# Summing the norms' squares on VectorE before one sum over the partitions, in a three-layer kernel on one core

## The chip, the cores and the metric

The kernel runs on one core of one Trainium2 chip. The metric is the device time of one execution in microseconds (us). TensorE multiplies matrices, VectorE (DVE in the profile) and ScalarE (ACT) work elementwise, GpSimd (POOL) and SyncE (SP) issue transfers here.

## The reference, cut to what matters

Three transformer layers work on one sequence of 256 tokens with 1024 features: stick-breaking attention, sparse attention over a latent with 16 heads, and window attention beside a gated linear recurrence. Each layer is followed by a feed-forward part with a causal convolution of three taps. Ahead of each half of a layer stands a norm over the features:

```python
y = xf * lax.rsqrt(jnp.mean(xf * xf, axis=-1, keepdims=True) + RMS_EPS)
h = rms_norm(x, norm_mix[i]) * (1.0 + sc1) + sh1
```

The sparse attention norms each of its 16 heads' queries over 128 features as well, and the window attention norms its output over 512 features. So the squares of x have to be summed over the features for every token, and the features lie on the partitions.

## The kernel before, in words

All activations are kept transposed: a tile holds 128 features on the partitions and T = 256 tokens along the free axis, and `x` is eight such tiles (`KT`). Weights stream in by DMA into `raw`; each piece is split into a high part `wh` on ScalarE (`high`) and a low part `wl` on VectorE (`low`), and each product is made of three in the float32r type (`three`): high by high, low by high, high by low. The activations are split likewise into `xh` and `xl`, `oh` and `ol`, `gh` and `gl`. A scheduler orders the instructions of each engine when the program is built; each engine then works through its own list in order.

`residual` stands at the end of each half of a layer. Its inner function `done` is called for the eight tiles in the order `ORD` (0, 2, 4, 6, 1, 3, 5, 7): VectorE adds the product to `x` (line 694), ScalarE makes `xh` (line 689) and the square `sq` (line 634), VectorE makes `xl` (line 690). After four tiles `gather` multiplies the four squares by `first_one`, a 128x32 tile whose first column is one, so that each product uses 32 columns of the array and leaves its sum over the partitions in one row of the bank `po`. After all eight, `regather` copies the bank to `part` on ScalarE (line 663) and multiplies it by `ones`, which yields one sum for each token. `rsqrt` takes these (line 647) through a logarithm, an exponential and one Newton step, and `spread` multiplies the result by the identity so that it stands on all partitions.

`opening` begins the next half of a layer meanwhile: its first three units take the split of x times its gain, without the norm's factor, and their results are scaled by the factor once it is there. `GS` says from which of these products on the sums and the spread must stand ahead of them in TensorE's list (lines 787 to 793).

The five norms handled in this way follow two kinds of half layers. Three follow an attention, so that `down_last` closes an output projection (the profile's stretches from 152, 499 and 842 us); two follow a feed-forward part (from 348 and 692 us). The very last norm (`last`, `finish`) already adds its squares on VectorE and isn't touched but for its buffers. In the sparse attention `heads` and `head_sums` do the same gathering for four groups of four heads, in the mixed layer `window` does it once.

Of the kernel before, what the change touches and what calls it, by code (L numbers as in the profile page):

```python
# [10 lines left out]
F32 = mybir.dt.float32  # L11
F32R = mybir.dt.float32r
U8 = mybir.dt.uint8
AF = mybir.ActivationFunctionType
# [16 lines left out]
# ---------------------------------------------------------------- layout of the inputs  # L31
# [172 lines left out]
# ---------------------------------------------------------------- the program  # L204
# [46 lines left out]
SQ = 5  # L251
# [20 lines left out]
class Prog:  # L272
# [22 lines left out]
    # -- small helpers  # L295
# [46 lines left out]
    # -- the weight stream: blocks come by DMA, pieces of them are split into two float32r parts ahead of use  # L342
# [139 lines left out]
    def heads_in_flight(self, n, st, ready, scores, middle, product, lag=2):  # L482
        """Heads in three stages, each a step or two behind the one before."""
        st.update(hold=False, out=False, done=0, open=0, ready=0, split=0)
        a = c = 0
        ticks = {}
        while st["done"] < n:
            can = a < n and not st["hold"] and ready(a) and a - c < (2 if st["out"] else 3)
            did = False
            if st["done"] + 1 < c and (st["done"] % 4 or not st["split"]):  # L490
                product(st["done"])
                st["done"] += 2
                did = True
            if c < a and (a - c >= 2 or not can) and self.tick - ticks[c] >= lag and c - st["done"] < WP:
                middle(c)
                c += 1
                did = True
            if can:
                scores(a)
                ticks[a] = self.tick  # L500
                a += 1
                did = True
            st["open"] = a - c
            yield did
# [6 lines left out]
    # -- conditioning  # L511
# [19 lines left out]
    def ada_pair(self, k):  # L531
        """The first layer's shift and gain of one tile of features."""
# [41 lines left out]
    # -- products with a block of the weights  # L574
# [56 lines left out]
    # -- residual and norm  # L631
    def square(self, src):
        sq = self.tmp.tile([128, T], F32, name="sq", bufs=SQ)
        self.sqi = self.nc.scalar.activation(sq, src, AF.Square).ins
        return sq
# [19 lines left out]

    def gather(self, p, sqs, start, stop):
        """Sums over the features of up to four tiles, each in a row of its own 32 columns of the array."""
        for j, sq in enumerate(sqs):
            self.gathered = self.mmul(p[32 * j:32 * j + 32, 0:T], self.first_one, sq, start, stop)

    def regather(self, p, o, rhs):
        part = self.tmp.tile([128, T], F32, name="part", bufs=1)
        self.nc.scalar.activation(part, p[:, 0:T], AF.Copy)
        for t in range(2):
            i = self.mmul(o(t), part[:, t * 128:t * 128 + 128], rhs, start=t == 0, stop=t == 1)
        return i
# [7 lines left out]
    def residual(self, L, h):  # L674
# [18 lines left out]
        def done(n, m, o):  # L693
# [6 lines left out]
            wait.append((self.square(self.x[:, m]), g))  # L700
            while len(wait) > (1 if n < KT - 1 else 0):
                sq, fn = wait.pop(0)
                if fn:
                    fn()
                sqs.append(sq)
                if len(sqs) % 4 == 0:
                    self.gather(self.np, sqs[-4:], len(sqs) == 4, len(sqs) == KT)
            if n == KT - 1:
                self.summed = self.regather(self.np, lambda t: self.np[:, t:t + 1], self.ones)

        sqs = []
# [23 lines left out]
    def opening(self, L, h, evacs):  # L735
        """Norm, modulation and the first three units: these take x before its norm, which then scales their result."""
# [45 lines left out]
        for half in range(2):  # L782
            k0 = 4 * half
            for i in range(n):
                wh, wl = self.next()
                for kk in range(4):
                    k = k0 + kk
                    for f in range(2):
                        g = 8 * i + 2 * kk + f
                        before = None if half or g < GS[0] else self.gathered if g < GS[1] else self.summed if g < GS[2] else spread  # L790
# [29 lines left out]
    # -- start  # L820
    def setup(self, sq, sv):
# [24 lines left out]
        self.first_one = keep.tile([128, 32], F32, name="first_one")  # L846
        nc.vector.memset(self.first_one, 0.0)
        nc.vector.memset(self.first_one[:, 0:1], 1.0)
# [86 lines left out]
    # -- feed forward with the causal convolution  # L935
# [69 lines left out]
    # -- layer 0: stick-breaking attention  # L1005
# [108 lines left out]
    # -- layer 1: sparse attention over a latent  # L1114
# [18 lines left out]
    def sparse(self, bias):  # L1133
        nc, I = self.nc, self.I
        blocks = ((0, slice(0, 128)), (1, slice(128, 384)))
        with ExitStack() as outer:
# [106 lines left out]
            def head_sums(g):  # L1243
                p = self.bank("small")
                self.gather(p, sqs[g], True, True)

                def rest():
                    self.regather(p, lambda t: p[:, 256 + 4 * t:260 + 4 * t], self.ident[:, ::32])
                    rqs[g] = sk.tile([128, 8], F32, name=f"rq{g}")
                    self.rsqrt(p[:, 256:264], 8, 128, rqs[g])  # L1250
                    ready.add(g)
                self.after(1, rest)

            def heads(g, u, b):
# [4 lines left out]
                sqs[g] += [self.square(b[:, j]) for j in range(2)]  # L1259
# [65 lines left out]
    # -- second block: window attention with sinks beside a gated linear recurrence  # L1325
    def mixed(self):
        nc, I = self.nc, self.I
        blocks = ((0, slice(0, 128)), (1, slice(128, 384)))
        with ExitStack() as outer:
# [149 lines left out]
            def window():  # L1479
                o = ao  # L1480
                cs = self.bank("po")
                self.gather(cs, [self.square(o[:, i]) for i in range(4)], True, True)
                yield True
                self.regather(cs, lambda t: cs[:, t:t + 1], self.ones)
# [219 lines left out]
```

## Time and profile before

| what | value |
|---|---|
| median of 3 runs | 1051.66 us (1051.03 to 1051.83) |
| profiled execution: span from the first to the last instruction | 1049.4 us |
| median less span (what lies around it) | 2.3 us |
| TensorE busy | 1031.3 us, 98% of the span |
| VectorE busy | 822.1 us, 78% |
| ScalarE busy | 646.2 us, 62% |

The profiled execution has no time of its own but its span; a run's time holds some 2.3 us more. An instruction's duration runs from its start to its end; matmuls overlap each other, so that what one costs is read from the distance between starts. A product in plain float32 stands in the trace as two records, so `x2` is one product and `x4` is two.

### The profile page before, as it was taken

What the parts mean: (1) busy time and instruction counts of PE and PEld (TensorE: products, weight loads), DVE (VectorE), ACT (ScalarE), POOL (GpSimd) and SP (SyncE); (2) the same over time, 40 slices, a digit from 0 to 9 for tenths busy, and PEclk for the clock granted to TensorE, in tenths of its full rate; (3) what the DMA queues carried; (4) which work ended last, traced back from release to release, by engine and by line L of the source; (5) the groups of instructions that cost most, each with busy time, mean ns of one, the idle gap of its engine ahead of it and who ended that gap; (6) DMA issues with size and microseconds to landing.
All of it is one profiled execution on the core that took longest, in us unless ns stands there. A gap on an engine that the chain in (4) does not pass through costs nothing.

```text
span 1049.4 us, 20050 instructions
## 1 busy us (share of the span) xinstructions
PE 1031.3 (98%) x8064; PEld 965.6 (92%) x8064; DVE 822.1 (78%) x1504; ACT 646.2 (62%) x1136; POOL 78.0 (7%) x148
## 2 busy tenths in 40 slices
PE   8999999999999999999999999999999999999997
PEld 5998889999999888867899999989888989999996
DVE  6955777999999689784798898877899679666664
ACT  6566648845555584775785555558786378445543
POOL 0003210011111010010000101000111000000000
PEclk9999999999999999999999999999999999999998
DMA  9958774588888285552367777746685325656531
GB/s 363 406 208 289 268 262 161 201 285 297 284 297 290 104 296 196 190 192 101 121 230 274 272 271 282 265 145 241 246 297 180 121 105 218 221 184 238 193 150 41
DMA packets 45791, 235.73 MB, mean 225 GB/s; under 512 B 5377, under 2 KB 6033, under 8 KB 28033
## 3 DMA queue, kind: packets, MB, share of 16 engines
q1 hardware_dynamic: 26066, 164.28, 42.7%
q0 software_dynamic: 19344, 69.78, 18.8%
q8 instruction: 63, 1.03, 0.4%
q10 hardware_dynamic: 288, 0.39, 0.1%
q14 instruction: 30, 0.25, 0.1%
HBM read 233.36 MB, written 1.07 MB: 223 GB/s over the span
## 4 chain that ended last, share of the span: by engine, by line
PE 96%; ACT 1%; DVE 1%; DMA 0%; issue 0%; DVEq 0%; SPq 0%
PE acc L301 39%; PE mm L301 35%; PE po L301 12%; PE small L301 10%; PE acc L1109 1%; DMA x<-xT 0%; DVE X L1543 0%; ACT X L327 0%; DVE adaw L528 0%; ACT pT L1111 0%; DVE xf L1668 0%; ACT lg L327 0%; DVE S L1564 0%; ACT lg L1291 0%; PE mm L1109 0%
## 5 line engine op out<-in xcount | busy, mean ns | idle before, releaser
L406 ACT ACTIVATE wh<-raw 128x1024 fp32r<-128x1024 f32 x290 | 304.6, 1057 | 234.2 <-PE acc L301 91.5
L418 DVE TENSOR_TENSOR wl<-raw,wh 128x1024 fp32r<-128x1024 f32 x290 | 352.6, 1221 | 98.0 <-PE mm L301 31.4
L301 PE MATMUL mm<-xl,wh 128*128 128x256 f32 (+1 forms) x872 | 247.1, 285 | 0.0
L301 PE MATMUL mm<-xh,wh 128*128 128x256 f32 (+1 forms) x872 | 246.1, 287 | 0.0
L301 PE MATMUL mm<-xh,wl 128*128 128x256 f32 (+1 forms) x872 | 245.6, 284 | 0.0
L528 DVE SCALAR_TENSOR_TENSOR adaw<-adaw,cond 128x1024 f32<-128x1024 f32 x144 | 174.5, 1217 | 10.5 <-DMA adaw<-ada 10.4
L301 PEld LDWEIGHTS mm<-xh,wh 128*128 128x128 f32 x872 | 163.3, 189 | 6.4 <-issue 4.7
L301 PEld LDWEIGHTS mm<-xl,wh 128*128 128x128 f32 x872 | 164.9, 189 | 4.6 <-DVE xl L690 2.5
L301 PEld LDWEIGHTS mm<-xh,wl 128*128 128x128 f32 x872 | 164.8, 189 | 1.6 <-issue 1.6
L301 PE MATMUL acc<-gl,wh 128*128 128x256 f32 x528 | 148.4, 282 | 0.0
L301 PE MATMUL acc<-gh,wl 128*128 128x256 f32 x528 | 148.0, 281 | 0.0
L301 PE MATMUL acc<-gh,wh 128*128 128x256 f32 x528 | 147.7, 282 | 0.0
L521 POOL DMA_DIRECT2D adaw<-ada x125 | 66.2, 530 | 787.5 <-DVE adaw L528 671.0
L301 PEld LDWEIGHTS acc<-gl,wh 128*128 128x128 f32 x528 | 99.5, 188 | 1.0 <-issue 0.8
L301 PEld LDWEIGHTS acc<-gh,wh 128*128 128x128 f32 x528 | 99.0, 188 | 0.8 <-DVE xl L690 0.8
L301 PEld LDWEIGHTS acc<-gh,wl 128*128 128x128 f32 x528 | 99.5, 188 | 0.0
L301 PE MATMUL small<-xh,wh 128*128 128x256 f32 x240 | 68.0, 283 | 0.0
L301 PE MATMUL small<-xl,wh 128*128 128x256 f32 x240 | 67.9, 283 | 0.0
L301 PE MATMUL small<-xh,wl 128*128 128x256 f32 x240 | 67.9, 283 | 0.0
L301 PE MATMUL po<-xh,wh 128*128 128x256 f32 x192 | 54.5, 284 | 0.0
L301 PE MATMUL acc<-xh,wh 128*128 128x258 f32 (+1 forms) x192 | 54.4, 293 | 0.0
L301 PE MATMUL po<-xl,wh 128*128 128x256 f32 x192 | 54.4, 283 | 0.0
(324 smaller groups left out, 2081.4 us busy)
## 6 DMA issues: line engine op xcount, KB each, us to landing
raw<-ffn SPq DMA_DIRECT2D x99, 1024.0 KB, 4.9
adaw<-ada POOLq DMA_DIRECT2D x125, 512.0 KB, 5.0
raw<-dsa SPq DMA_DIRECT2D x15, 1024.0 KB, 5.0
raw<-hg SPq DMA_DIRECT2D x15, 1024.0 KB, 4.8
adaw<-ada SPq DMA_DIRECT2D x19, 512.0 KB, 10.2
raw<-sb SPq DMA_DIRECT2D x16, 512.0 KB, 10.2
raw<-sb SPq DMA_DIRECT2D x8, 1024.0 KB, 6.1
bias<-scr POOLq DMA_DIRECT2D x8, 256.0 KB, 5.4
```

The source lines that it names most:

```text
L301: return self.nc.tensor.matmul(o, a, b, start=start, stop=stop, skip_group_check=True).ins
L406: inst = nc.scalar.activation(h[:, :k * n], self.raws[b][:, c0:c0 + k * n], AF.Copy).ins
L418: inst = nc.vector.tensor_tensor(l[:, :k * n], self.raws[b][:, c0:c0 + k * n], h[:, :k * n], op=ALU.subtract).ins
L521: self.nc.gpsimd.dma_start(raw, self.I[f"ada{L}"][b])
L528: return self.nc.vector.scalar_tensor_tensor(w, w, 1.0, self.cond[n // 24], op0=ALU.mult, op1=ALU.mult, accum_out=self.M[n // 12][:, n % 1 ...
L1109: nc.tensor.transpose(b[:, i * 128:(i + 1) * 128], p[:, i * 128:(i + 1) * 128], self.ident)
```

## The change

The squares are taken for two tiles of x at a time, in one instruction over 512 elements (`squares`). VectorE adds the four results of a norm into the first (`add`, three additions in place), and the sum over the partitions is taken once: four products with the one column of `ones` (`sums`). `gather`, `regather`, `first_one` and `part` are gone. The buffers of `sq` are 3 of 512 elements rather than 5 of 256. In the sparse attention the squares come in pairs of heads, and each head's sum is taken with `ones` right away, eight products for a group of four heads; the step of `head_sums` that stood one turn later is gone. In `window` one addition joins the two squares, and four products sum them.

```diff
-SQ = 5
+SQ = 3
...
+    def squares(self, src):
+        sq = self.tmp.tile([128, 2, T], F32, name="sq", bufs=SQ)
+        self.sqi = self.nc.scalar.activation(sq, src, AF.Square).ins
+        return sq
...
-    def gather(self, p, sqs, start, stop):
-        for j, sq in enumerate(sqs):
-            self.gathered = self.mmul(p[32 * j:32 * j + 32, 0:T], self.first_one, sq, start, stop)
-
-    def regather(self, p, o, rhs):
-        part = self.tmp.tile([128, T], F32, name="part", bufs=1)
-        self.nc.scalar.activation(part, p[:, 0:T], AF.Copy)
-        for t in range(2):
-            i = self.mmul(o(t), part[:, t * 128:t * 128 + 128], rhs, start=t == 0, stop=t == 1)
-        return i
...
-            wait.append((self.square(self.x[:, m]), g))
+            wait.append((n, g))
             while len(wait) > (1 if n < KT - 1 else 0):
-                sq, fn = wait.pop(0)
+                i, fn = wait.pop(0)
                 if fn:
                     fn()
-                sqs.append(sq)
-                if len(sqs) % 4 == 0:
-                    self.gather(self.np, sqs[-4:], len(sqs) == 4, len(sqs) == KT)
+                if i % 2:
+                    add(i)
             if n == KT - 1:
-                self.summed = self.regather(self.np, lambda t: self.np[:, t:t + 1], self.ones)
+                for j in range(2):
+                    self.summed = self.sums(self.np[:, 0:2], self.total[:, j], j == 0, j == 1)
+
+        def add(i):
+            j, k = ORD[i - 1:i + 1]
+            sq = self.squares(self.x[:, j:k + 1:k - j])
+            if i == 1:
+                self.total = sq
+            else:
+                nc.vector.tensor_tensor(self.total, self.total, sq, op=ALU.add)
...
-                        before = None if half or g < GS[0] else self.gathered if g < GS[1] else self.summed if g < GS[2] else spread
+                        before = None if half or g < GS[1] else self.summed if g < GS[2] else spread
...
-                self.gather(p, sqs[g], True, True)
-
-                def rest():
-                    self.regather(p, lambda t: p[:, 256 + 4 * t:260 + 4 * t], self.ident[:, ::32])
-                    rqs[g] = sk.tile([128, 8], F32, name=f"rq{g}")
-                    self.rsqrt(p[:, 256:264], 8, 128, rqs[g])
-                    ready.add(g)
-                self.after(1, rest)
+                for j, sq in enumerate(sqs[g]):
+                    self.sums(p[:, 256 + j:264:4], sq, j == 0, j == 3)
+                rqs[g] = sk.tile([128, 8], F32, name=f"rq{g}")
+                self.rsqrt(p[:, 256:264], 8, 128, rqs[g])
+                ready.add(g)
...
-                self.gather(cs, [self.square(o[:, i]) for i in range(4)], True, True)
+                sq, other = [self.squares(o[:, i:i + 2]) for i in (0, 2)]
+                nc.vector.tensor_tensor(sq, sq, other, op=ALU.add)
                 yield True
-                self.regather(cs, lambda t: cs[:, t:t + 1], self.ones)
+                for j in range(2):
+                    self.sums(cs[:, 0:2], sq[:, j], j == 0, j == 1)
```

The scheduler lays the lists anew. On TensorE, at the end of the first layer's attention (the stretch from 152 us), two of the places where a gathering product stood before, between the last products of the output projection (`oh`, `ol`) and the first ones of the opening (`xh`, `xl`):

```order
L301 MATMUL acc<-oh,wl 128x256
L301 MATMUL po<-sq,first_one 32x256
L301 MATMUL mm<-xl,wh 128x258
L301 MATMUL mm<-xh,wl 128x258
L301 MATMUL mm<-xl,wh 128x258
L301 MATMUL mm<-xh,wl 128x258
L301 MATMUL po<-sq,first_one 32x256 x2
L301 MATMUL mm<-xh,wh 128x258 x2
L301 MATMUL po<-sq,first_one 32x256
```

Now no product of the norm stands there; the first one is the sum over the partitions, four products in one piece, ahead of the same product of the opening as `part` stood before:

```order
L301 MATMUL mm<-xh,wh 128x258
L301 MATMUL mm<-xl,wh 128x258
L301 MATMUL po<-ones,sq 128x1 x4
L301 MATMUL acc<-xh,wh 128x258
L301 MATMUL acc<-xl,wh 128x258
```

The eight gathering products of this norm stood in five places, and are gone; the two products with `part` became the four with `sq`.

On VectorE, at the same end of an attention, the list after the fourth of the eight additions to x was this before; `wl` is the low part of the next weights, `rs` the first step of the norm's factor:

```order
L694 SCALAR_TENSOR_TENSOR x<-acc,mod_176,x 128x256
L418 TENSOR_TENSOR wl<-raw,wh 128x1024
L690 SCALAR_TENSOR_TENSOR xl<-x,gain_179,xh 128x256 x3
L418 TENSOR_TENSOR wl<-raw,wh 128x1024
L647 TENSOR_SCALAR rs_1729<-po 128x2
```

and is this now, from one addition to x earlier:

```order
L687 SCALAR_TENSOR_TENSOR x<-acc,mod_173,x 128x256
L710 TENSOR_TENSOR sq<-sq 128x512
L687 SCALAR_TENSOR_TENSOR x<-acc,mod_173,x 128x256
L418 TENSOR_TENSOR wl<-raw,wh 128x1024
L683 SCALAR_TENSOR_TENSOR xl<-x,gain_176,xh 128x256 x3
L710 TENSOR_TENSOR sq<-sq 128x512
L683 SCALAR_TENSOR_TENSOR xl<-x,gain_176,xh 128x256
L418 TENSOR_TENSOR wl<-raw,wh 128x1024
L710 TENSOR_TENSOR sq<-sq 128x512
L652 TENSOR_SCALAR rs_1713<-po 128x2
```

The three additions of squares are in the list, and the last of them stands behind both pieces of `wl`.

At the end of a feed-forward part (the stretch from 348 us) VectorE's list now has the last addition ahead of the second `wl`:

```order
L687 SCALAR_TENSOR_TENSOR x<-acc,mod_173,x 128x256
L1143 SCALAR_TENSOR_TENSOR gqk<-vec 128x1
L418 TENSOR_TENSOR wl<-raw,wh 128x1024
L710 TENSOR_TENSOR sq<-sq 128x512
L683 SCALAR_TENSOR_TENSOR xl<-x,gain_177,xh 128x256 x2
L710 TENSOR_TENSOR sq<-sq 128x512
L418 TENSOR_TENSOR wl<-raw,wh 128x1024
L652 TENSOR_SCALAR rs_4096<-po 128x2
```

Here one `wl` less is ahead of the sum than at the end of an attention.

## Rows read from the trace of the kernel before

**Rows 1.** The profile's page: span, TensorE's busy time, the chain that ended last.
```profile
span 1049.4 us, 20050 instructions
...
PE 1031.3 (98%) x8064; PEld 965.6 (92%) x8064; DVE 822.1 (78%) x1504; ACT 646.2 (62%) x1136; POOL 78.0 (7%) x148
...
PE 96%; ACT 1%; DVE 1%; DMA 0%; issue 0%; DVEq 0%; SPq 0%
```

**Rows 2.** Gathering products alone, by stretch: length, busy time of PE, PEld, DVE.
```profile
152.00:174.00 22.00, 3.12 (x16) 0.71 (x16) 0.00 (x0) 1.00 0.29 111
348.00:372.00 24.00, 4.34 (x16) 0.97 (x16) 0.00 (x0) 1.00 0.26 90
399.00:404.00 5.00, 1.86 (x8) 0.42 (x8) 0.00 (x0) 1.00 0.82 292
...
793.00:796.00 3.00, 1.25 (x8) 0.29 (x8) 0.00 (x0) 1.00 0.89 277
```

**Rows 3.** TensorE in order of time around single and threefold gathering products.
```profile
156.18 0.28 PE L301 MATMUL acc<-oh,wl 128*128 128x256 f32 x1
156.39 0.62 PE L301 MATMUL po<-sq,first_one 128*32 128x256 f32 x2
156.94 0.38 PE L301 MATMUL acc<-oh,wh 128*128 128x256 f32 x1
157.16 0.28 PE L301 MATMUL acc<-ol,wh 128*128 128x256 f32 x1
...
162.23 0.63 PE L301 MATMUL po<-sq,first_one 128*32 128x256 f32 x6
162.79 0.39 PE L301 MATMUL acc<-xh,wh 128*128 128x258 f32 x1
```

**Rows 4.** TensorE in order of time around sums with one column.
```profile
164.82 0.28 PE L301 MATMUL mm<-xl,wh 128*128 128x258 f32 x1
164.94 0.50 PE L301 MATMUL po<-ones,part 128*128 128x1 f32 x4
165.30 0.37 PE L301 MATMUL acc<-xh,wh 128*128 128x258 f32 x1
165.51 0.28 PE L301 MATMUL acc<-xl,wh 128*128 128x258 f32 x1
...
821.29 1.52 PE L301 MATMUL small<-ones,sq 128*128 128x1 f32 x12
822.67 0.36 PE L301 MATMUL acc<-oh,wh 128*128 128x256 f32 x1
```

**Rows 5.** VectorE at the end of the first attention, and its 128x512 addition-like form.
```profile
153.28 1.66 DVE L694 SCALAR_TENSOR_TENSOR x<-acc,mod,x 128x256 f32<-128x256 f32 x4 [0.61 <-PE acc L301]
...
158.01 0.47 DVE L694 SCALAR_TENSOR_TENSOR x<-acc,mod,x 128x256 f32<-128x256 f32 x1
158.41 1.21 DVE L418 TENSOR_TENSOR wl<-raw,wh 128x1024 fp32r<-128x1024 f32 x1
159.54 1.27 DVE L690 SCALAR_TENSOR_TENSOR xl<-x,gain,xh 128x256 fp32r<-128x256 f32 x3
...
L970 DVE TENSOR_TENSOR yg<-yg,yv 128x512 f32<-128x512 f32 x22 | 15.0, 684 | 0.0
```

**Rows 6.** The end of the first feed-forward part: VectorE's first additions, TensorE's sums.
```profile
346.72 1.66 DVE L694 SCALAR_TENSOR_TENSOR x<-acc,mod,x 128x256 f32<-128x256 f32 x3 [0.96 <-PE acc L301]
348.30 0.48 DVE L690 SCALAR_TENSOR_TENSOR xl<-x,gain,xh 128x256 fp32r<-128x256 f32 x1
...
360.81 0.50 PE L301 MATMUL po<-ones,part 128*128 128x1 f32 x4
```

**Rows 7.** Stretches of the sparse attention and the recurrence: PE, PEld, DVE, ACT, POOL.
```profile
400.00:453.00 53.00, 53.00 (x377) 44.15 (x373) 43.21 (x127) 32.60 (x82) 2.64 (x5) 1.00 0.52 180
453.00:464.00 11.00, 9.88 (x60) 6.68 (x59) 9.03 (x32) 8.53 (x29) 2.11 (x4) 1.00 0.54 189
...
760.00:812.00 52.00, 50.22 (x389) 44.85 (x390) 46.98 (x107) 38.13 (x94) 7.93 (x15) 1.00 0.70 243
```

More of the change, by code (lines that the diff above doesn't have):

```diff
@@ L629, in down_last @@
             done(n, m, self.acc(m))
+    def squares(self, src):
+        sq = self.tmp.tile([128, 2, T], F32, name="sq", bufs=SQ)
+        self.sqi = self.nc.scalar.activation(sq, src, AF.Square).ins
+        return sq
     def square(self, src):
-        sq = self.tmp.tile([128, T], F32, name="sq", bufs=SQ)
+        sq = self.tmp.tile([128, 2, T], F32, name="sq", bufs=SQ)[:, 0]
         self.sqi = self.nc.scalar.activation(sq, src, AF.Square).ins
@@ L699, in done @@
             g = gain(m) if after else None
-            wait.append((self.square(self.x[:, m]), g))
+            wait.append((n, g))
             while len(wait) > (1 if n < KT - 1 else 0):
-                sq, fn = wait.pop(0)
+                i, fn = wait.pop(0)
                 if fn:
                     fn()
-                sqs.append(sq)
-                if len(sqs) % 4 == 0:
-                    self.gather(self.np, sqs[-4:], len(sqs) == 4, len(sqs) == KT)
+                if i % 2:
+                    add(i)
             if n == KT - 1:
-                self.summed = self.regather(self.np, lambda t: self.np[:, t:t + 1], self.ones)
-        sqs = []
+                for j in range(2):
[7 more added lines that the diff above has]
+                nc.vector.tensor_tensor(self.total, self.total, sq, op=ALU.add)
         def last(n, m):
@@ L845, in setup @@
         nc.vector.memset(self.ones, 1.0)
-        self.first_one = keep.tile([128, 32], F32, name="first_one")
-        nc.vector.memset(self.first_one, 0.0)
-        nc.vector.memset(self.first_one[:, 0:1], 1.0)
         self.negones = sv.tile([128, 128], F32, name="negones", bufs=1)
@@ L1258, in heads @@
                 nc.scalar.activation(qs[g][:, 2 * u:2 * u + 2], b, AF.Copy)
-                sqs[g] += [self.square(b[:, j]) for j in range(2)]
+                sq = self.squares(b)
+                sqs[g] += [sq[:, j] for j in range(2)]
                 if u:
```

## Prediction, made before the changed kernel ran

> **What bounds the kernel now.** I read the page first, then the busy time by stretches, then the order of time around the norms. TensorE is busy for 1031.3 of 1049.4 us, and 96% of the chain that ended last is TensorE [rows 1]. The reader is to see in this that TensorE's list is the clock of this kernel: an instruction taken out of it brings its own time, unless what stands behind it then waits for another engine. Two views tell where that can be. The stretches of the sparse attention and of the recurrence show where TensorE idles already: not at all from 400 to 453 us (53.00 of 53.00), 1.1 us from 453 to 464, and 1.8 us from 760 to 812, where VectorE is busy for 46.98 of 52 [rows 7]. And the order of time around a norm shows what VectorE does while the norm is under way [rows 5, 6]: it isn't idle there, it has sixteen operations on x and xl and the low parts of the next weights to do.
>
> **What is removed from TensorE.** A bulk product follows the one before it after 0.12 us (164.82 to 164.94) [rows 4]. A single gathering product between two of them costs much more than its columns suggest: from 156.18 to 157.16 are 0.98 us, two bulk steps among them, so that the break costs 0.98 - 0.24 = 0.74 us. Three gathering products in one place take 0.56 us to the next product where one took 0.55 [rows 3]. So the price goes by the place, not by the product. One place is busy for 0.62 us [rows 3], so that the busy times by stretch count the places: 3.12 / 0.62 = 5 after the first attention, 4.34 / 0.62 = 7 after the first feed-forward part, 3 for the first group of heads, 2 for the window attention [rows 2]. The three norms after an attention are laid alike, as are the two after a feed-forward part, and the four groups of heads. That is 3.7 us of breaks in each of three norms, 5.2 us in each of two, 2.2 us in each of four groups, 1.5 us in the window attention. `part` costs 164.82 to 165.51 less two steps, 0.45 us, at each of these ten places [rows 4].
>
> The Trainium skill, page "TensorEngine Tiling (Array Packing)", sections "Theoretical Speedup" and "Key Properties", speaks against a gain: it says that tiles of 32 columns run beside each other and bring up to four times, while a change of the tiling mode drains the engine. The trace agrees with both halves: three run in the time of one, and every place where they stand alone costs the 0.74 us. By the fourfold alone, the eight products of a norm would cost two places, 1.5 us, and the change would bring 1.5 + 0.45 - 0.9 = 1.0 us a norm and lose 0.6 us a group of heads (0.74 + 0.45 - 1.83), some 2.5 us in all; by the places as the rows count them it is what I work out here.
>
> **What is added to TensorE.** Two one-column products cost 0.45 us, and twelve records (six products) take 1.38 us, 0.115 us a record [rows 4]. Four products are eight records: 0.45 + 4 x 0.115 = 0.91 us for a norm. Eight products for a group of heads: 0.45 + 12 x 0.115 = 1.83 us. TensorE alone is thus relieved of 3.7 + 0.45 - 0.91 = 3.2 us in three norms, 5.2 + 0.45 - 0.91 = 4.7 us in two, 2.2 + 0.45 - 1.83 = 0.84 us in four groups, 1.0 us in the window attention: 9.7 + 9.5 + 3.4 + 1.0 = 23.6 us. That is the upper bound.
>
> **What is added to VectorE, and where it ends last.** Each of the five norms gets three additions of 128x512. The same form on the feed-forward part's tiles takes 0.684 us [rows 5]; the trace has no other value for it, and I take it whole, 2.05 us a norm. They stand in a list that is full. After an attention, VectorE starts the additions to x at 153.28 [rows 5]. Ahead of the norm's sum its list now has eight additions to x and eight xl, each 0.395 us from start to start (158.01 to 158.41 shows 0.40), two wl of 1.13 us (158.41 to 159.54), and the three additions: 153.28 + 6.32 + 2.26 + 2.05 = 163.9. TensorE, rid of 3.7 us, would be there at 164.94 - 3.7 = 161.2. So TensorE waits there, some 2.7 us in all, at the sum or a little ahead of it for a low part of the weights that comes later too. The sum starts 1.0 us earlier than the one of before did, and it is 0.46 us longer: **0.55 us a norm, 1.6 us for three**, not 9.7. Behind the sum the factor, the spread and the products of the opening are the same chain as before.
>
> After a feed-forward part one wl less stands ahead of the last addition. VectorE's first three additions to x take until 348.30 there, since they wait for TensorE [rows 6]. Then come thirteen of 0.395 us, one wl and three additions: 348.30 + 5.14 + 1.13 + 2.05 = 356.6. TensorE would be there at 360.81 - 5.2 = 355.6, so it waits 1 us. The sum moves from 360.81 to 356.6 or so, 4.2 us, less 0.46: **3.7 us a norm, 7.4 us for two**.
>
> The squares cost ScalarE less, four instructions rather than eight and no `part`; it isn't what ends last here, and I take nothing for that. With three buffers the last square of a norm needs the buffer of the second, which the first addition frees; that is some operations earlier.
>
> **The groups of heads** add nothing to VectorE. The first three lie where TensorE never idles [rows 7], so that their 0.84 us count whole; of the fourth I take half, since there TensorE waits for the heads now and then: **3.0 us**. The lists of this stage are laid anew over hundreds of rows, which could give or take some; the bounds are 0 and 4.5 (all of 3.4, and the 1.1 us that TensorE idles from 453 to 464).
>
> **The window attention** lies where VectorE is busy for 90% and TensorE has room [rows 7]. TensorE's 1.0 us and VectorE's addition of 0.68 us stand against each other; I take 0, with 0.7 us of loss and 1.0 of gain as bounds.
>
> **The sum:** 1.6 + 7.4 + 3.0 = 12.0 us. The profiled span 1049.4 becomes 1037.4; the median of the runs lies 2.3 us above the span, so the time is 1039.7 us.
>
> **Rivals.** (1) *VectorE doesn't hold the sum*: its additions are cheaper in the list than I take them, or fall into its waits, and all 23.6 us come: 1028 us. For it speaks that TensorE is nearly all of the chain [rows 1]; against it that the list after an attention is full from 153.28 on [rows 5]. (2) *VectorE holds it longer*: each of the additions waits for its square or the next low part besides, 1.2 us a norm more. Then three norms lose 0.65 us each, two gain 2.5 us each, and the heads give nothing: 3.0 us, 1048.7 us. (3) *The gathering products cost little*: they only filled a wait, since the norm's factor and spread set the end of those stretches anyway (no change, 1051.7 us), or four of them are done in the time of one, two places a norm (2.5 us by the prices above, 1049.2). For it speaks that three cost what one does; against it that bulk products stand step by step on both sides of a single one, and that the places are many [rows 2, 3]. (4) *Slower*: in the sparse attention's new order the transposes of a head's weights stand too early on TensorE, ahead of the softmax that makes them. From 453 to 464 TensorE already idles for 1.1 us [rows 7]. If each of 16 heads lost 1 us more, that would be 16 us against the 9.0 us of the norms: 1058.7 us. It decides from 0.55 us a head on. For it speaks that the whole stage is laid anew; against it that TensorE has bulk products to put between, as it does up to 453.
>
> **How the numbers follow.** My forecast has 0.62, rival 1 0.10, rival 2 0.13, rival 3 0.07, rival 4 0.08. A difference of 0.2%, 2.1 us, is about what can be told from no change here. Rivals 1 and 2 are faster too, by more than that, so faster has 0.85, the same 0.07, slower 0.08. The range of my forecast is that of its unknown costs: 12.0 - 3.0 - 0.7 - 3 (half of rival 2's cost in each norm) = 5 us saved at least, and 12.0 + 1.5 + 1.0 + 6 (of the 19.2 - 9.0 = 10.2 that VectorE holds back in the five norms) = 21 us at most: 1031 to 1047. Most of rivals 1, 3 and 4 and part of 2 lie outside, so the range stays there.
>
> **What would show it.** Right: no product with 32 columns, and in each norm's stretch TensorE waits for VectorE ahead of the one-column products; after an attention the sum starts 10.6 us behind the first addition to x (before: 164.94 - 153.28 = 11.7), and after a feed-forward part 9.9 us behind it (before: 360.81 - 346.72 = 14.1). The additions of squares take some 0.68 us. Wrong: TensorE doesn't wait at the sums (rival 1), or the sums start later than these (rival 2), or waits of TensorE for the heads' weights grow over the sparse attention (rival 4).

## The result, and the profile after

The changed kernel takes 1033.32 us (median of four runs, 1032.43 to 1033.52) against 1051.74 us before: a ratio of 0.982, 95% interval 0.980 to 0.984. The gain is 18.4 us where I forecast 12.0, inside the range of 1031 to 1047. The profiled execution took 1033.22 us, with a span of 1031.4 us against 1049.4. What lies around the span is thus 1.8 us, not the 2.3 us that I took from a median and another execution's span; the forecast went by the difference, so that nothing hangs on it.

The page of the profile after, to be held against [rows 1]: span, busy time of the engines, chain that ended last.

```profile
span 1031.4 us, 19934 instructions
...
PE 1006.4 (98%) x8016; PEld 964.0 (93%) x8016; DVE 831.3 (81%) x1518; ACT 640.2 (62%) x1096; POOL 78.0 (8%) x148
...
PE 91%; DVE 6%; ACT 1%; DMA 0%; issue 0%; DVEq 0%; SPq 0%
```

TensorE lost 24.9 us of busy time, VectorE gained 9.2, and VectorE's share of the chain went from 1% to 6%: at some places TensorE now waits for it. Where, the first norm shows. In order of time, VectorE's and then TensorE's instructions behind the first attention (answers to [rows 3 to 5]):

```profile
152.60 1.66 DVE L687 SCALAR_TENSOR_TENSOR x<-acc,mod,x 128x256 f32<-128x256 f32 x4 [0.61 <-PE acc L301]
...
157.93 1.22 DVE L418 TENSOR_TENSOR wl<-raw,wh 128x1024 fp32r<-128x1024 f32 x1
159.06 1.28 DVE L683 SCALAR_TENSOR_TENSOR xl<-x,gain,xh 128x256 fp32r<-128x256 f32 x3
160.25 0.69 DVE L710 TENSOR_TENSOR sq<-sq 128x512 f32<-128x512 f32 x1
160.85 0.48 DVE L683 SCALAR_TENSOR_TENSOR xl<-x,gain,xh 128x256 fp32r<-128x256 f32 x1
161.25 1.22 DVE L418 TENSOR_TENSOR wl<-raw,wh 128x1024 fp32r<-128x1024 f32 x1
162.38 0.69 DVE L710 TENSOR_TENSOR sq<-sq 128x512 f32<-128x512 f32 x1
```

```profile
159.20 0.51 PE L301 MATMUL acc<-xh,wl 128*128 128x258 f32 x2 [1.48 <-DVE wl L418]
...
162.21 0.29 PE L301 MATMUL mm<-xl,wh 128*128 128x258 f32 x1
163.22 1.02 PE L301 MATMUL po<-ones,sq 128*128 128x1 f32 x8 [0.72 <-DVE sq L710]
164.10 0.37 PE L301 MATMUL acc<-xh,wh 128*128 128x258 f32 x1
...
165.97 0.61 PE L301 MATMUL po<-ident,rs 128*128 128x128 f32 x4
```

The reader is to see VectorE's list without a gap from 157.93 to the last addition of squares, and TensorE waiting for it twice: 1.48 us for a low part, 0.72 us ahead of the one-column products. That is 2.2 us of the 2.7 us that the prediction gave for this wait. The sum starts 163.22 - 152.60 = 10.62 us behind the first addition to x; the prediction said 10.6, before it was 11.7. After the first feed-forward part (answer to [rows 6]):

```profile
344.97 1.68 DVE L687 SCALAR_TENSOR_TENSOR x<-acc,mod,x 128x256 f32<-128x256 f32 x3 [0.96 <-PE acc L301]
...
354.10 0.69 DVE L710 TENSOR_TENSOR sq<-sq 128x512 f32<-128x512 f32 x1
...
352.57 1.99 ACT L406 ACTIVATE wh<-raw 128x1024 fp32r<-128x1024 f32 x2
...
354.61 0.39 PE L301 MATMUL mm<-xh,wh 128*128 128x258 f32 x1 [0.89 <-ACT wh L406]
...
355.19 0.95 PE L301 MATMUL po<-ones,sq 128*128 128x1 f32 x8
```

The sum starts 10.22 us behind the first addition (forecast 9.9, before 14.1), and TensorE's wait here is not for VectorE: it waits 0.89 us for ScalarE's second high part of the weights (done at 354.56), and four bulk products stand between that wait and the sum. VectorE's last addition is done at 354.79, 0.4 us ahead of the sum. In the fourth norm TensorE waits 0.49 us for a low part of VectorE and 0.22 us for a high part of ScalarE, and nowhere at the sum.

I took the same three marks at all five norms (first addition to x, sum, first spread product) and so cut the span into stretches. From first addition to spread the norms became 0.52, 3.41, 0.53, 3.43 and -0.38 us shorter, 7.5 together. From the second norm's spread to the third norm's first addition, the sparse attention, 363.05 to 498.18 became 357.89 to 485.81: 7.2 us. From the fourth norm's spread to the fifth norm, the recurrence and the window attention: 1.0 us. The start before the first norm gives 0.7 us, the three feed-forward stretches 0.54, 0.54 and 0.10, the end 0.4. Together 18.0, the difference of the spans. (The start holds the same work in all kernels here, and took 152.0 to 154.8 us in their profiles, so that its 0.7 is no effect. The five longest, runs 1, 4, 8, 10 and 11, are those in which TensorE's granted clock fell to half for 3.4 or 6.8 us from 68 to 70 us on.)

The fifth norm is the odd one. The start of its sum, then TensorE's granted clock around it, by windows (behind the length: busy time of PE, PEld, DVE, ACT, POOL, then the clock):

```profile
833.70 1.05 PE L301 MATMUL po<-ones,sq 128*128 128x1 f32 x8 [1.34 <-DVE sq L710]
```

```profile
832.00:834.00 2.00, 0.66 (x6) 0.45 (x5) 1.65 (x2) 0.00 (x0) 0.00 (x0) 1.00 0.00 0
834.00:835.00 1.00, 1.00 (x10) 1.00 (x10) 0.16 (x1) 0.01 (x1) 0.00 (x0) 1.00 0.00 0
835.00:836.00 1.00, 1.00 (x7) 1.00 (x7) 0.47 (x4) 0.97 (x3) 0.00 (x0) 0.56 0.00 0
836.00:837.00 1.00, 1.00 (x7) 1.00 (x6) 1.00 (x2) 0.37 (x1) 0.00 (x0) 0.50 0.00 0
837.00:838.00 1.00, 1.00 (x6) 1.00 (x6) 0.15 (x1) 0.00 (x0) 0.00 (x0) 0.50 0.06 16
838.00:839.00 1.00, 1.00 (x8) 1.00 (x8) 0.00 (x0) 0.32 (x1) 0.00 (x0) 0.73 0.80 131
```

TensorE waited 1.34 us for the last addition of squares there, and 1.4 us behind the sum's start its clock was granted at half, 1.2 in place of 2.4 GHz, for some 3 us. A bulk product takes 0.215 us from start to start in it, not 0.12, and the spread comes 837.58 - 833.70 = 3.88 us behind the sum, where the other norms have 2.7. The next stretch still has 0.5 us of it: the last feed-forward part took 178.8 us here and 178.3 in runs 3, 6, 7, 9 and 10. In runs 3, 10 and 11, which leave this norm's sum as it is, TensorE waited the same 1.3 us and its clock did not fall; there the spread comes 2.8 us behind the sum. So the change alone doesn't decide the half clock.

(The lists of VectorE under "The change" begin with the eighth addition to x before, and with the seventh now, not with the fourth.)

### The profile page after: what moved, and what is told of

Same layout as the page of the kernel before. It is cut to its first block, busy times and chain, and to the rows that moved or that the text cites. A ratio compares the mean times of both kernels' runs of the same rounds, so it can differ in the third digit from the quotient of the medians.

```text
span 1031.4 us, 19934 instructions
## 1 busy us (share of the span) xinstructions
PE 1006.4 (98%) x8016; PEld 964.0 (93%) x8016; DVE 831.3 (81%) x1518; ACT 640.2 (62%) x1096; POOL 78.0 (8%) x148
## 4 chain that ended last, share of the span: by engine, by line
PE 91%; DVE 6%; ACT 1%; DMA 0%; issue 0%; DVEq 0%; SPq 0%
PE acc L301 37%; PE mm L301 33%; PE po L301 11%; PE small L301 10%; DVE x L687 1%; DVE xl L683 1%; DVE X L1539 1%; PE acc L1105 1%; DVE sq L710 1%; DVE wl L418 1%; DVE adaw L528 1%; DMA x<-xT 0%; DVE S L1560 0%; ACT wh L406 0%; DVE xf L1664 0%
## 5 line engine op out<-in xcount | busy, mean ns | idle before, releaser
L301 PE MATMUL acc<-xh,wl 128*128 128x258 f32 (+1 forms) x192 | 53.0, 287 | 3.5 <-DVE wl L418 3.5
L301 PE MATMUL acc<-xl,wh 128*128 128x258 f32 (+1 forms) x192 | 54.3, 286 | 0.0
L301 PE MATMUL acc<-oh,wh 128*128 128x256 f32 x192 | 52.8, 292 | 1.5 <-ACT oh L333 0.9
```

Source lines behind the costliest of these rows:

```text
L301: return self.nc.tensor.matmul(o, a, b, start=start, stop=stop, skip_group_check=True).ins
```

## Experiments

Times are medians; each ratio is to the kernel before, run beside it on the same chip, with its 95% interval. "The stage" is the stretch of the sparse attention named above, 135.1 us before and 127.9 after.

**1. The norms alone.** Gathering products, `part` and the later turn go back into the heads and the window attention; their squares still come in pairs, as in the changed kernel.

```diff
 def head_sums(g):
-    for j, sq in enumerate(sqs[g]):
-        self.sums(p[:, 256 + j:264:4], sq, j == 0, j == 3)
+    self.gather(p, sqs[g], True, True)
+    def rest():
+        self.regather(p, lambda t: p[:, 256 + 4 * t:260 + 4 * t], self.ident[:, ::32])
...
+    self.after(1, rest)
```

> The change with the gathering products, the later turn and `part` back in the heads and in the window attention; only the norms keep the new sums. My forecast gives the norms 9.0 us (1042.7 against 1051.7 before); the profile after shows 7.5 us in the five stretches, 1044.2. Rival, the gain is elsewhere and the norms' stretches only shift it: 1049 or more. Rival, VectorE does not hold the sum: 19.2 us, 1032.5.

1042.18 us, 0.991 (0.990 to 0.992): 9.3 us less than before. The trace gives the five norms 7.2 us of it, and the stage 2.5, since with squares in pairs a group's gathering products stand in two places and not in three: four places fewer, 3.0 us by 0.74 us each. In this trace the clock fell at the third norm as well as at the fifth.

**2. The heads alone**, in the kernel before: their four squares summed by eight one-column products each, factor in the same turn.

> The kernel before with only the groups of heads changed: their squares are summed by eight one-column products and the factor follows in the same turn; norms and window attention as before. My forecast gives 3.0 us, 1048.7. The profile after shows 7.2 us in this stage, which would be 1044.5. If the stage gains only together with the norms (a stage that starts in another order), 1051.

1043.63 us, 0.993 (0.992 to 0.995): 7.8 us less, the stage 127.75 us. So the heads gain by themselves more than twice my 3.0 us, without the norms. With run 1's 6.8 us, those 2.5 left out that lie in the heads, this makes 14.6 of the 18.4 us.

**3 and 4. The turn.** Run 3 is the changed kernel with the heads' factor one turn later again; run 4 is the kernel before with `part` and the factor in the same turn.

```diff
-    rqs[g] = sk.tile([128, 8], F32, name=f"rq{g}")
-    self.rsqrt(p[:, 256:264], 8, 128, rqs[g])
-    ready.add(g)
+    def rest():
+        rqs[g] = sk.tile([128, 8], F32, name=f"rq{g}")
+        self.rsqrt(p[:, 256:264], 8, 128, rqs[g])
+        ready.add(g)
+    self.after(1, rest)
```

> The changed kernel, with the factor of a group of heads again one turn behind its sums. If the products alone bring the sparse stage's 7.2 us, it stays at 1033.3. If the earlier turn brings the part that I did not forecast, 4.2 us come back: 1037.5.

> The kernel before, gathering products and all, with `part` and the factor of a group of heads in the same turn as its gathering products. If the earlier turn brings 4.2 us by itself: 1047.5. If it is the products that matter, 1051.7; if TensorE then waits for `part` in each of four groups (ScalarE's copy of a bank in between), some 2 us more, 1053.7.

Run 3: 1033.64 us, 0.983 (0.982 to 0.984), the stage 128.4 us: the turn is worth nothing beside one-column products. Run 4: 1049.61 us, 0.999 (0.998 to 1.000), by its interval not to be told from no change; its stage took 133.3 us in the trace, 1.8 less than before.

**5. One more operation on VectorE** in each norm, ahead of the sum, with no effect on its value.

```diff
     nc.vector.tensor_tensor(self.total, self.total, sq, op=ALU.add)
+    if i == KT - 1:
+        nc.vector.tensor_tensor(self.total, self.total, sq, op=ALU.max)
```

(The total contains these squares as one of its terms, so the larger of the two is the total. The expectation says "itself" for this operand.)

> The changed kernel with one more 128x512 operation on VectorE in each norm, behind the last addition of squares (the larger of the total and itself, which leaves the total as it is). If VectorE holds each norm's sum, each of the five norms gets 0.6 us longer: 1036.3, a little more where TensorE's clock falls behind the longer wait. If VectorE's list does not hold it (TensorE or ScalarE's squares do), 1033.3.

1054.56 us, 1.002 (1.001 to 1.003): 21 us more than the changed kernel, not 3. The sums behind an attention start 11.34, 11.34 and 11.25 us behind the first addition, each some 0.72 us later, as expected; behind a feed-forward part 11.61 and 12.13. But from first addition to spread the norms are 0.7, 3.4, 1.3, 3.0 and 1.9 us longer, with the clock at half behind the last four, and the recurrence's stage is 7.8 us longer (140.2 against 132.4): the additional instructions had moved rows of TensorE, VectorE and ScalarE there. TensorE's waits in that stage (what it waited for, us, times, longest), and windows from 780 to 820 us:

```profile
PE acc L301 <- DVE S L1562: 3.0, 2, 1.8
```

```profile
780.00:800.00 20.00, 16.57 (x128) 14.85 (x128) 18.77 (x43) 9.00 (x28) 3.17 (x6) 0.96 0.69 230
800.00:820.00 20.00, 19.90 (x124) 19.64 (x124) 10.87 (x26) 10.87 (x22) 0.00 (x0) 0.70 0.09 32
```

Two waits of TensorE for the recurrence's state S, and then 20 us at a mean clock of 0.70. This run mixes a price with a new order, so it can't give the price; run 10 repeats it without the new order.

**6. The second low part behind the last addition of squares.** In the rows of the first norm above, the second `wl` (161.25) stands ahead of the last addition (162.38), though the third unit needs it only behind the spread.

```diff
-    self.low(i0 + 2, self.lastx if GW else None)
+    self.low(i0 + 1, self.lastx if GW else None)
+    self.low(i0 + 2, self.lastadd)
```

> The changed kernel, with the second of two low parts of the weights in an attention's norm placed behind the last addition of squares, where it stood ahead of it. If VectorE holds the sum, the sum's total is there 1.1 us earlier and the 0.7 us that TensorE waits at the sum go, in each of three norms; where the clock fell to half, 1.2 us more: 1030.0 to 1031.2. If the low part is then late for the third unit, the wait only moves: 1033.3 or more.

1029.24 us, 0.979 (0.978 to 0.981): 4.1 us faster than the changed kernel, the fastest of this study. VectorE and TensorE in its first norm:

```profile
160.63 0.68 DVE L710 TENSOR_TENSOR sq<-sq 128x512 f32<-128x512 f32 x1
...
161.23 1.22 DVE L418 TENSOR_TENSOR wl<-raw,wh 128x1024 fp32r<-128x1024 f32 x1
...
161.60 0.29 PE L301 MATMUL mm<-xl,wh 128*128 128x258 f32 x1
161.73 0.95 PE L301 MATMUL po<-ones,sq 128*128 128x1 f32 x8
```

No wait ahead of the sum, which starts 9.75 us behind the first addition (151.98) and not 10.62. From first addition to spread the three norms behind an attention are 0.95, 0.92 and 2.24 us shorter, 4.1 in all; the two behind a feed-forward part are as they were. The third of these no longer meets the half clock, and 1.1 of its 2.24 us is that; runs 3, 10 and 11 got this 1.1 back with the fifth norm untouched. What the moved low part brings by itself is thus some 3.0 us, 1.0 us a norm.

**7. The last pair summed by TensorE**: three tiles of squares added on VectorE, the fourth summed by four products of its own.

```diff
+    elif i == KT - 1:
+        self.pair = sq
     else:
         nc.vector.tensor_tensor(self.total, self.total, sq, op=ALU.add)
```

> The changed kernel with the last pair of squares not added on VectorE: TensorE sums it by four products of its own, eight in place of four. If VectorE holds the sum after an attention, the sum can start at the end of the addition before, 2.2 us earlier, and is 0.46 us longer: about 1.4 us in each of three norms, against 0.45 us lost in each of the two after a feed-forward part: 1030.0. If TensorE's own work decides, 0.45 us lost in each of five: 1035.6.

1030.57 us, 0.980 (0.979 to 0.981): 2.7 us faster, near the 3.3 expected, but not where I had put it. The sums start 9.27, 8.58, 9.27, 7.90 and 8.47 us behind the first addition, 1.4 to 2.3 earlier; the spreads come 0.04, 0.28, 0.02, 0.34 and 1.84 us earlier. TensorE's order puts four more bulk products between sum and spread (nine in the fourth norm) and the sum itself is 0.9 us longer, so the lead is used up; 1.84 of the 2.5 us lie in the fifth norm, and 1.1 of them are again its clock.

**8. The old gathering products, four by four**, in the kernel before: each waits for the last square made by then, which is the fifth for the first four products and the eighth for the others.

```diff
     self.gathered = self.mmul(p[32 * j:32 * j + 32, 0:T], self.first_one, sq, start, stop)
+    if late:
+        self.behind(self.gathered, late)
...
-    self.gather(self.np, sqs[-4:], len(sqs) == 4, len(sqs) == KT)
+    self.gather(self.np, sqs[-4:], len(sqs) == 4, len(sqs) == KT, self.sqi)
```

> The kernel before with the norms' gathering products four by four: each waits for the last square of its four, so that they stand in two places (in places next to each other after the first attention) and not in five or seven. By the place, 0.74 us each: 2.2 us less in each of three norms, 3.7 us in each of two, 14.0 us in all, 1037.7. By the product, nothing: 1051.7. If they only filled a wait for the factor, 1051.7 too.

1042.28 us, 0.991 (0.990 to 0.993): 9.3 us less than before, of 14.0 expected by the place. The five norms bring 10.6 us in the trace; its start is 1.5 us longer, with the clock at half from 68 us on. TensorE's gathering products around the first and the second norm:

```profile
159.12 0.64 PE L301 MATMUL po<-sq,first_one 128*32 128x256 f32 x8
159.69 0.50 PE L301 MATMUL mm<-xh,wh 128*128 128x258 f32 x2
160.12 1.76 PE L301 MATMUL po<-sq,first_one 128*32 128x256 f32 x8
161.81 0.39 PE L301 MATMUL acc<-xh,wh 128*128 128x258 f32 x1
...
352.43 0.64 PE L301 MATMUL po<-sq,first_one 128*32 128x256 f32 x8
355.36 0.64 PE L301 MATMUL po<-sq,first_one 128*32 128x256 f32 x8
```

Four products in one place are busy for 0.64 us, as one is for 0.62 [rows 3]. Behind a feed-forward part, two places in place of seven bring the sum forward from 14.08 to 10.40 us behind the first addition, 3.68 us, and TensorE waits for nothing on the way in either kernel; five places at 0.74 are 3.7. Behind an attention the second place lasts 161.81 - 160.12 = 1.69 us, 1.12 more than the other, because its later products wait for their squares; 2.2 - 1.1 is the 1.1 us measured there (11.66 to 10.56). So the price goes by the place, and the norms' part of the change could be had on TensorE alone, with no addition on VectorE: 10.6 us in the five stretches here, 7.2 to 7.5 there.

**9. The first low part earlier too**, on top of run 6: behind the fifth addition to x.

```diff
+    if n == 4:
+        self.fifth = self.lastx
...
-    self.low(i0 + 1, self.lastx if GW else None)
+    self.low(i0 + 1, self.fifth)
```

> The kernel of the sixth run (second low part behind the last addition of squares), with the first low part, for which TensorE waits 1.48 us in each of three norms, placed behind the fifth addition to x and not behind the eighth. If VectorE's list as a whole sets the sum, that wait only moves to the sum: VectorE's last addition of squares ends 0.4 us ahead of the sum now, so at most 0.4 us in each of three norms, 1028.0 to 1029.2. If the low part itself is what holds TensorE, 1.48 us in each of three: 1024.8.

1030.79 us, 0.980 (0.979 to 0.981): 1.5 us slower than run 6, and neither of the expected times. TensorE's waits in the first norm, from 151 to 166 us:

```profile
PE mm L301 <- DVE xl L683: 1.5, 1, 1.5
```

The wait only moved, from the low part to an xl that now stands behind it on VectorE. The sum starts 9.48 us behind the first addition (run 6: 9.75), but the new order puts more bulk products behind it, and the spread comes 12.73 us behind (12.43). The edit reaches all five norms, and each is 0.2 to 0.5 us longer than in run 6.

**10. Run 5's operation in the first and third norm only.**

> The changed kernel with the extra 128x512 operation of VectorE in the first and third norm only, so that the recurrence's stage keeps its order up to its last part. If VectorE holds those sums, 0.72 us each, as the fifth run's trace shows: 1034.7, up to 1.3 us more for each norm in which the clock falls behind the wait. If the 21 us of the fifth run come with every such operation, some 4 us each: 1041.7.

1036.12 us, 0.985 (0.984 to 0.986): 2.8 us more than the changed kernel. Its first norm, VectorE and TensorE:

```profile
163.54 0.68 DVE L710 TENSOR_TENSOR sq<-sq 128x512 f32<-128x512 f32 x1
164.26 0.69 DVE L712 TENSOR_TENSOR sq<-sq 128x512 f32<-128x512 f32 x1
...
165.10 0.69 PE L301 MATMUL po<-ones,sq 128*128 128x1 f32 x5 [1.43 <-DVE sq L712]
```

TensorE's wait at the sum grows from 0.72 to 1.43 us, and both sums start 0.72 us later: what VectorE gets is what the sum is late. In the first norm that is all (spread 0.74 us later); in the third the spread is 2.3 us later, with the clock at 0.60 from 500 to 504 us. The waits were the same in both, 1.5 and 1.4 us. The fifth norm, as in the changed kernel, met no half clock here and was 1.1 us shorter; the start was 1.2 us longer.

**11. The heads with gathering products in two places, factor in the same turn**, in the changed kernel.

> The changed kernel with the heads' gathering products back (in two places a group, since their squares come in pairs) and with `part` and the factor in the same turn. By the prices of single products this is 2 x 0.74 + 0.45 = 1.93 us a group against 1.83: 1033.7. If the order of the heads' stage decides, and with gathering products it stays as in the first run (132.7 us from the second spread to the third norm against 127.9), 1038.0; with the turn's share that the fourth run showed, 1.8 us less: 1036.2.

1040.66 us, 0.991 (0.989 to 0.992): 7.3 us slower than the changed kernel, where single prices said 0.4, and more than any of the three expected times. The stage took 131.5 us, 3.6 more; the recurrence's stage 2.0 more, with the same instructions in another order; the fifth norm met no half clock and was 1.1 shorter; the rest lies in the start, which was 1.5 us longer with the clock at half for a while, and in what run 12 shows.

**12. A tile that nobody reads.** All profiles with the tile `first_one` in the kernel had the first feed-forward stretch at 179.5 to 179.6 us, all without it at 179.0, with the same products.

```diff
 nc.vector.memset(self.ones, 1.0)
+self.first_one = keep.tile([128, 32], F32, name="first_one")
+nc.vector.memset(self.first_one, 0.0)
+nc.vector.memset(self.first_one[:, 0:1], 1.0)
```

> The changed kernel with the 32-column tile `first_one` kept and filled as before, though nothing reads it: no instruction of TensorE or ScalarE is moved, but the tiles allocated behind it lie 128 bytes a partition further on. In all six profiles with this tile in the kernel the first stretch from a norm's spread to the next norm took 179.5 to 179.6 us, in the seven without it 179.0 us, with the same products. If the place of the tiles in the memory does it, this kernel takes 179.5 us there and some 2.3 us more in all, 1035.6. If the products on quarter arrays do it (or chance), 179.0 us and 1033.3.

1037.23 us, 0.986 (0.984 to 0.988): 3.9 us slower than the changed kernel. 179 us of the first feed-forward part, first of this run, then of the changed kernel:

```profile
168.00:347.00 179.00, 179.00 (x1496) 178.81 (x1496) 162.71 (x262) 110.15 (x152) 14.80 (x28) 1.00 0.80 276
```

```profile
166.00:345.00 179.00, 179.00 (x1501) 178.81 (x1500) 162.91 (x262) 109.97 (x152) 14.80 (x28) 1.00 0.79 276
```

1496 products against 1501, 0.3% in pace, both at full clock; the stretch itself takes 179.5 us again. The three feed-forward stretches and the recurrence's are each some 0.5 us longer, 2.0 us. TensorE and ScalarE work through the same lists in both kernels. The rest of the profile's 4.7 us is the start (0.5), the second norm, which met the half clock (0.7), and the sparse attention behind it (1.4, of which the rest of that half clock can hold 0.8).

## Why the prediction was right, and where it was off

**Breaks by the place.** Right. Run 8 changed only where the gathering products stand and got 3.68 us for five places, 0.74 each. The Trainium skill, page "TensorEngine Tiling (Array Packing)", section "Key Properties", says that changing the tiling mode drains the engine; run 8 agrees, with four products at 0.64 us a place and the price in the places; that it is a drain no run shows.

**VectorE holds the sum.** Right behind an attention, and shown: the walk through its list gave 10.6 us where 10.62 was measured; run 10 delayed VectorE by one operation and the sum by 0.72 us; run 6 took 1.1 us of other work from ahead of the last addition, and the sum came 0.87 us earlier, where TensorE was the later one. That the walk fits to 0.02 us is luck: in the list an addition delays the next instruction by 0.60 us only (160.25 to 160.85), not by the 0.684 that I took, which made the walk 0.16 us too long, and the 0.15 us from the last addition's end (163.07) to the sum (163.22) were not in it. Behind a feed-forward part the wait was put to the wrong engine. VectorE's last addition is done 9.82 us behind the first addition to x, near the 9.9 walked, but no wait stands at the sum: in the second norm TensorE waits last for ScalarE's high part of the weights, 0.89 us, and of ScalarE I had written "it isn't what ends last here". The two ends lie a quarter of a microsecond apart (354.56 and 354.79), so the 3.7 us came out near in spite of it; that is luck too, and no run shows what VectorE's additions alone cost there. Rival 1 falls, since no sum comes earlier than walked by more than 0.1 us, and rival 2 too: none is later by more than 0.3 us.

**The terms for the norms.** 0.52 and 0.53 us behind an attention (forecast 0.55), 3.41 and 3.43 behind a feed-forward part (3.7). The fifth norm should have gained 0.55 and lost 0.38. What failed there is the sentence that behind the sum "the factor, the spread and the products of the opening are the same chain as before": the clock fell behind the new wait, and the chain ran at half speed, 1.1 us longer. I had priced TensorE's waits by their length alone. Without that fall this norm gains 0.7 us, as runs 3, 10 and 11 show. So the norms brought 7.5 us in place of 9.0.

**The groups of heads: the mis-sized term.** 3.0 us forecast; 7.8 measured by themselves (run 2), 7.2 in the changed kernel's stage. Both lie outside the bounds that I gave the term. These bounds, 0 and 4.5, came from the sums' own products, and these were right: three places, 0.74 each, and `part`. What I missed is in the sentence that the lists laid anew "could give or take some", which I bounded by TensorE's idle time. From one product's start to the next, TensorE spent in the stage before and after: on the transposes of the heads' attention weights 8.1 and 5.8 us, on their products with the latent 11.9 and 11.0, on the scores 9.8 and 8.7, on the masks 5.4 and 5.1 (sums over the stage's 192 products of these four kinds). That is 4.5 us on products that the change doesn't touch, which the 3.0 lacked. A part of it is waiting, TensorE's waits for ScalarE's copy of a head's transposed attention weights. Over the stage, in the kernel before, then in the changed one:

```profile
PE po L301 <- ACT pT L1111: 2.2, 4, 0.6
```

```profile
PE po L301 <- ACT pT L1107: 0.6, 1, 0.6
PE acc L301 <- ACT pT L1107: 0.6, 1, 0.6
```

Two waits fewer, 1.0 us. A good part of the 4.5 is seen in single long steps. More than 0.45 us from one product's start to the next, the gathering products' own left out, passed eleven times before (7.1 us in all) and passes five times in the changed kernel (3.4 us); nine or ten times (5.6 to 6.9 us) in runs 1, 4 and 11, six or seven times (4.4 us) in runs 2 and 3. Seven of the eleven steps, and two of the five, end at a product with the latent, which needs that copy. So the wait that rival 4 feared would grow was there before, and shrank. Three orders with one-column products took 127.8 to 128.4 us (runs 2 and 3, and the change; the stages of runs 5 and 12, 129.2 and 129.3 us, began at half clock), four with gathering products 131.5 to 135.1 (runs 1, 4 and 11, and before). The earlier turn isn't it: run 3 gave it back and lost 0.3 us. Run 11 says that it isn't the products' own price either, since that predicts 0.4 us where 3.6 stood in the stage. That the order laid around them does it is what is left, and is argued: no run kept the order and changed the products. Why the new order has fewer of these steps stays open.

**The window attention.** 0 forecast. The stretch of the recurrence and the window attention took 132.4 us in the changed kernel and 132.7 to 132.9 in runs 3, 6, 7, 9 and 10, which have the same window attention, against 133.3 in run 1, which has the gathering products there beside the new norms, and 133.4 before. Run 1 has the tile of run 12 too, which costs 0.5 us in this stretch. So 0 to 0.5 us are left for the window attention, inside my bounds and no more than orders of this stretch differ by.

**What I had no term for.** `first_one` went with the gathering products, and the place of every later tile moved by 128 bytes a partition. Run 12 prices this at 2.0 us of pace, 0.5 in each of the three feed-forward stretches and in the recurrence's, in a kernel in which nothing reads the tile; in the trace of the change it is the 0.54 us in each of two feed-forward stretches and about half of the recurrence's 1.0, while in the third feed-forward stretch the half clock takes back 0.5. Rivals 3 and 4 have nothing for them: the products cost what they did, and TensorE's waits in the sparse stage became fewer.

In the trace of the change, then, the sum of 12.0 was long by 1.5 (the norms: 0.9 in the fifth, 0.6 in the other four) and short by 4.2 (heads), 1.0 (the recurrence and the window attention, tiles included), 1.2 (the feed-forward stretches) and 1.1 (start and end): 18.0, the difference of the spans. The time stayed inside the range because the range was wide, 16 us, and not because each term was inside its own bounds.

## What to carry to other kernels

A small product that switches the array's layout between bulk products is paid for by the place: before replacing such products by work on another engine, bring them together; for the norms it gave as much here, with no engine loaded more. Where work is moved to an engine whose list is full, look at once for what stands in that list ahead of the last operation and isn't needed yet: one such instruction in each of three norms (run 6) was worth 3.0 us, and 4.1 with the clock that no longer fell. And where a planner lays the order, a few added instructions can move a stage by several microseconds (run 5: 7.8), so that a price is taken from the stretch of the trace, and not from the total.

## What the runs showed of the hardware

TensorE's granted clock fell to 0.50, 1.2 GHz, behind waits of 0.9 to 3 us in all in stretches of otherwise dense work, for some 3 us (in run 5 up to 14). It fell without a wait too: in five of the fourteen profiles at 68 to 70 us, behind some 4 us of mostly 64x256 products (`acc<-qk`), while the other nine ran the same products at full clock. Where it can be told apart, a fall cost some 1.6 us: 1.5 in run 10's third norm (2.3, less the 0.72 of the added operation), 1.1 and 0.5 behind it in the changed kernel's fifth. The waits did not decide it: in run 10 the first and the third norm had the same two (1.5 and 1.4 us), and only the third fell; the second norm waited 0.9 us in the changed kernel and in run 12, and fell only in run 12; the norms of run 9 waited 1.0 to 1.6 us each, and none fell. The Trainium skill, page "TensorE: Matmul & The Clock Gate", section "What's actually happening", says that the monitor runs free of the kernel's start, so that the point of a change varies; these runs agree with that, and none tests it.

The pace of identical bulk products differed by 0.3 to 0.4% between kernels whose tiles lie 128 bytes a partition apart: 119.7 against 119.2 ns from start to start in the feed-forward stretches, the same in each of the seven profiles with the unread or read tile and in each of the seven without. No run shows what in the address does it.
